# A two-layer HGRN2 / RWKV-7 decoder step: gates, scores and chain in another order, narrower sample products, memory operands split sooner

## The chip, the cores and the metric

One Trainium2 chip, one of its cores. The metric is the device time of one execution in microseconds (us), lower is better. The kernel before takes 2398.97 us (median of 3 runs, 2397.93 to 2401.8).

## What is computed

A trunk of two layers over 1024 prompt tokens and 64 sample tokens (8 sequences of 8), model width 1024, in fp32:

```
layer 0: h = rmsnorm(x); q, f, v, xq, gate = h @ w_in[0]
         HGRN2, 8 heads of 128: S = exp(b_last)*S + (k*exp(b_last-b)) v ;  o = att v + (q*exp(b)) S
layer 1: h = rmsnorm(x); shifted mixes xr, xw, xk, xv, xa = h + (h_prev - h)*mu
         RWKV-7, 16 heads of 64:  S = S*w + (S a) b + v k ;  y = S r
both:    xo = softmax(xq mem_k) mem_v over 256 memory tokens, 4 heads
         x = x + ([mixer | xo] * silu(gate)) @ w_out
mem_k, mem_v = rmsnorm(mem_prompt) @ w_mem_kv  (for the prompt; the samples have caches)
```

Outputs are both token groups after a final norm, the recurrent states and the memory keys and values.

## The kernel before, in words

Big products are made from fp32 operands split into a high and a low part (`split`, L194 to L200: ScalarE (ACT) rounds the high part at L197, VectorE (DVE) or GpSimd (POOL) subtracts at L200), and three matmuls on TensorE (PE) per tile (L216 to L218, or L242 and L1163 to L1165). `load_w` (L203) loads a weight block in one DMA on the SP queue (L209) and splits it. Each call of a tile pool names its buffers; instructions are put into one queue per engine at build time by a list scheduler, which takes program order as the priority and a modelled clock for what is ready. So program order, `tc.high_priority()` and the buffer counts (`BF`, `RB1`) set the order of the work; at run time each engine takes its queue strictly in order.

The stages, by the trace of the profiled execution:

- 0 to 149 us: `build_hT` norms and transposes the tokens of layer 0 (L254 to L269), and the value projection runs beside it: four blocks of 256 columns, each weight block one load and one split by ACT and POOL.
- 149 to 236 us: `memory_kv` (L273). For each of the two layers: transpose the normed memory (L290), scale by DVE (L291), split into `memh` and `meml` (one buffer each; low part by POOL), then eight weight blocks of 128 columns (low part by POOL and DVE in turn) and their products.
- 236 to 858 us: eight HGRN heads (`hgrn_head`, `hgrn_half`). After head h comes the gate of head h-1, then what `FILL[h]` lists: cross attention of the prompt (x), of samples (s), gates 8 to 11 (g). The sample part of a head (L737 to L764) multiplies each sequence's 8 queries with its state (L744), copies the result to SBUF, adds it to the output through a product with the identity (L750), and updates the states in two groups of four sequences: `vx` masks the values of all 64 tokens (L758), one product with 64 rows and 512 columns each (L762), DVE adds (L763).
- 858 to 1050 us: output projection of layer 0 (`out_proj`, L890), its weights loaded at L834.
- 1050 to 1472 us: layer 1's mixes (`blend`, L1038, L1039), low-rank products, and the key, value and receptance projections. `proj` (L1125) runs `key_direction` (L1309 to L1346) of block j after the products of block j+1: it squares, splits (`sh`, `sl`), sums over a head by PE (L1334, L1335) and takes a Newton step of four DVE operations (L1339 to L1342). The value projection opens each PSUM bank by a product with zeros (`zb`, L1156).
- 1472 to 1745 us: `PLAN` and `PLAN2` (L43): twelve gates (g), four cross heads (x), four sample steps (s), and the preparation, scores, tokens, inverse and merge (p, c, t, i, m) of the first blocks.
- 1745 to 2205 us: the loop over nine blocks of `RSEQ` (block 0, the sample block, blocks 1 to 7). Per turn n (L1251): `chain` of block n under high priority, the recurrence itself (L1643 to L1708); `merge_steps` (five, L1560) of block n+1 woven 1 to 2 with `score_steps` (eight, L1461, L1464) of block n+2; then `tokens` (L1489) and `inverse` (L1525 to L1542, a substitution of 15 DVE pairs, L1534 and L1535) of block n+2, `pre` of block n+3, `out` of block n-1, `sample_out`. In turn 0 `sample_in` (L1617) brings the samples' states in, through one PSUM buffer.
- 2205 to 2400 us: the last chain, and the output projection of layer 1.

`rstd_of` (L168) is the norm's reciprocal root: two ACT steps and four DVE operations (L178 to L181) after L173. The lines that set the loop's order:

```
PLAN  "x0 g0 x1 x2 g1 x3 g2 s0 g3 s1 g4 p0 c0 s2 g5 s3"   PLAN2 "t0 i0 m0 p1 g6 g7 g8 g9 g10 g11"
with tc.high_priority():
    x.chain()
ops(n + 1, "values")
weave(seq[n + 1].merge_steps(), seq[n + 2].score_steps(), *WV)      # WV = (1, 2)
ops(n + 2, "tokens", "inverse")
ops(n + 3, "pre")
```

Of the kernel before, what the change touches and what calls it, by code (L numbers as in the profile page):

```python
# [18 lines left out]
D = 1024  # L19
# [24 lines left out]
    "x0 g0 x1 x2 g1 x3 g2 s0 g3 s1 g4 p0 c0 s2 g5 s3", "t0 i0 m0 p1 g6 g7 g8 g9 g10 g11")]  # L44
# [3 lines left out]
WV = (1, 2)  # L48
# [6 lines left out]
BF = dict(hs=3, oT=3, qk=3, zn=3, lt=4, kb=2, tot=2, vv=3, cmp=2, kt=1, S=6, oi=1, kts=1, S0=2, vx=1)  # L55
# [112 lines left out]
def rstd_of(g, ss, n, scale, eps, p=128, sm=None):  # L168
# [9 lines left out]
    nc.vector.tensor_mul(t[:p, :n], y[:p, :n], y[:p, :n])  # L178
    nc.vector.tensor_mul(t[:p, :n], t[:p, :n], v[:p, :n])
    nc.vector.tensor_scalar(t[:p, :n], t[:p, :n], -0.5, 1.5, op0=ALU.mult, op1=ALU.add)  # L180
    nc.vector.tensor_mul(y[:p, :n], y[:p, :n], t[:p, :n])  # L181
# [21 lines left out]
def load_w(g, pool, src, w, kt=KT, elo="pool", raws=2):  # L203
# [5 lines left out]
    nc.sync.dma_start(out=raw, in_=src.rearrange("(k p) c -> p k c", p=128))  # L209
    split(g, hi, lo, raw, elo=elo)  # L210
# [58 lines left out]
def memory_kv(g, mp, sp, kT0, v0):  # L269
# [6 lines left out]
    for i in range(2):  # L276
        x = sp("mx")[:, :D]
        nc.sync.dma_start(out=x, in_=g.mem_prompt[0, 128 * i:128 * i + 128, :])
        norm_rows(g, xs[i], x, 128)
    for layer in range(2):  # L280
        mh = mp.tile([128, KT, MEM], F32R, name="memh", tag="memh", bufs=1)
        ml = mp.tile([128, KT, MEM], F32R, name="meml", tag="meml", bufs=1)
        gb = g.vec[:, g.vo["mg"] + layer * KT:g.vo["mg"] + (layer + 1) * KT]
        for i in range(2):
# [9 lines left out]
            split(g, mh[sl], ml[sl], h)  # L294
# [6 lines left out]
        for j in range(8):  # L301
            w = load_w(g, mp, g.w_mem_kv[layer, :, 128 * j:128 * j + 128], 128, elo="dve" if j % 2 else "pool", raws=3)
# [128 lines left out]
def hgrn_masks(g, c):  # L431
    nc = g.nc
    si = c.tile([128, 32], I32, name="si")
    ti = c.tile([128, 32], I32, name="ti")
    xi = c.tile([128, 32], I32, name="xi")
# [4 lines left out]
    a = c.tile([128, 32], F32, name="ma")  # L440
    b = c.tile([128, 32], F32, name="mb")
    u = c.tile([128, 32], F32, name="mu_")
# [5 lines left out]
    for n, h in enumerate((2, 4, 8, 16)):  # L448
# [3 lines left out]
        nc.vector.tensor_mul(lev[:, n, :], a, u)  # L452
    return base, lev
# [17 lines left out]
def hgrn_layer(ctx, g):  # L471
# [14 lines left out]
    with pool(g, "vw", 2, "right") as vw:  # L486
        with pool(g, "bh", 1) as bh:
            build_hT(g, xsrc, 0, hi, lo, bh)
        for c in range(4):
            wh, wl = load_w(g, vw, g.w_in[0, :, 2048 + 256 * c:2048 + 256 * c + 256], 256)  # L490
# [10 lines left out]
    with pool(g, "xk", 1, "right") as xk:  # L501
# [7 lines left out]
        with pool(g, "hm", 1, "right") as hm, pool(g, "h2", 1, "right") as h2, pool(g, "xc", 1, "right") as xc, \  # L509
# [3 lines left out]
            mbase, mlev = hgrn_masks(g, hm)  # L513
# [459 lines left out]
def rwkv_layer(ctx, g, nn, left):  # L973
# [151 lines left out]
    def proj(col0, cols, xh, xl, dst, fn, after=None, gemm=gemm_ko, raws=2):  # L1125

        late = None
        for j in cols:
# [13 lines left out]
            if late:  # L1142
                after(*late)
# [709 lines left out]
```

## Time and profile before

| | us |
|---|---|
| runs | 2397.93, 2401.8, 2398.97 |
| the profiled execution, and its span from first to last instruction | 2401.76, 2399.8 |
| PE busy, PE weight loads busy | 2238.2, 2001.5 |
| DVE, ACT, POOL busy | 1332.2, 1004.3, 717.7 |
| mean granted clock of TensorE | 0.934 of full speed |

PE is the busiest engine; its busy time also grows where its clock is granted at half speed (1.2 in place of 2.4 GHz), so busy share and granted clock are read together. A matmul record overlaps the next, so the cost of one in a stream is the distance between starts. A row of the timeline gives start, length, engine, line, operation and count, and in brackets the idle time before it and what ended it.

### The profile page before, as it was taken

Reading aid. Unit: us, or ns where it says so; the run is one execution under the profiler, and the core shown is the slowest. Engines: PE = TensorE matmul, PEld = TensorE weight load, DVE = VectorE, ACT = ScalarE, POOL = GpSimd, SP = SyncE. Lnnn points to the kernel's source line nnn. Section 1 sums busy time; section 2 is a strip of 40 time slices with the busy share of each in tenths; the row PEclk is TensorE's granted clock in tenths of the full one; section 3 lists DMA queues with packets and bytes.
Section 4 is the critical chain, followed back from the end, with each engine's and each line's share of the span. In section 5 each row is a group of like instructions: output and inputs, shape, how many; then the busy total and the mean of one; then the engine's idle time right before and its main releaser. Section 6 shows DMA issues by size and latency. Waiting matters only on the chain. (4 is left out here: it accounts for less than half of the span.)

```text
span 2399.8 us, 50625 instructions
## 1 busy us (share of the span) xinstructions
PE 2238.2 (93%) x20980; PEld 2001.5 (83%) x20981; DVE 1332.2 (56%) x2678; ACT 1004.3 (42%) x2240; POOL 717.7 (30%) x559
## 2 busy tenths in 40 slices
PE   5988999999999979989989998999999998899997
PEld 5988888888788858878979998898889987788786
DVE  6113566556775553365796214245576589874643
ACT  4222444444444442266554313344544455444421
POOL 2123121122112310034553412113143255444432
PEclk9998999999999989999999998999986798887999
DMA  5334111223432264215434425145332233312653
GB/s 184 86 96 142 48 56 45 67 70 91 111 87 87 80 193 127 84 41 199 148 122 163 127 93 145 50 103 134 113 108 72 57 101 99 90 55 82 201 158 105
DMA packets 360312, 252.99 MB, mean 105 GB/s; under 512 B 120379, under 2 KB 326403, under 8 KB 360083
## 3 DMA queue, kind: packets, MB, share of 16 engines
q1 hardware_dynamic: 348034, 237.66, 33.3%
q0 software_dynamic: 2544, 7.64, 0.9%
q10 hardware_dynamic: 9504, 4.46, 0.7%
q8 instruction: 165, 2.70, 0.5%
q14 instruction: 65, 0.52, 0.1%
HBM read 172.59 MB, written 77.11 MB: 104 GB/s over the span
## 5 line engine op out<-in xcount | busy, mean ns | idle before, releaser
L200 POOL TENSOR_TENSOR wlo<-wraw,whi 128x1024 fp32r<-128x1024 f32 (+1 forms) x84 | 214.9, 2560 | 646.5 <-ACT whi L197 623.8
L216 PE MATMUL pg<-hi,whi 128*128 128x288 f32 (+3 forms) x800 | 269.1, 336 | 4.5 <-DVE qk L597 2.3
L218 PE MATMUL pg<-hi,wlo 128*128 128x288 f32 (+3 forms) x800 | 266.0, 333 | 0.0
L217 PE MATMUL pg<-lo,whi 128*128 128x288 f32 (+3 forms) x800 | 265.9, 332 | 0.0
L197 ACT ACTIVATE whi<-wraw 128x1024 fp32r<-128x1024 f32 (+1 forms) x92 | 101.0, 1099 | 178.5 <-issue 104.9
L216 PEld LDWEIGHTS pg<-hi,whi 128*128 128x128 f32 x800 | 153.8, 192 | 21.5 <-issue 4.4
L217 PEld LDWEIGHTS pg<-lo,whi 128*128 128x128 f32 x800 | 153.7, 192 | 12.9 <-issue 3.1
L218 PEld LDWEIGHTS pg<-hi,wlo 128*128 128x128 f32 x800 | 153.5, 192 | 11.8 <-issue 2.3
L890 PE MATMUL pout<-owh,bh 128*128 128x512 f32 (+1 forms) x432 | 143.1, 397 | 9.2 <-ACT owh L197 9.2
L890 PE MATMUL pout<-owl,bh 128*128 128x512 f32 (+1 forms) x432 | 142.0, 394 | 0.1
L890 PE MATMUL pout<-owh,bl 128*128 128x512 f32 (+1 forms) x432 | 141.2, 394 | 0.9 <-DVE bl L200 0.9
L216 PE MATMUL pg<-xhi,whi 128*128 128x384 f32 (+2 forms) x392 | 127.6, 325 | 7.1 <-DVE evs L1136 5.0
L218 PE MATMUL pg<-xhi,wlo 128*128 128x384 f32 (+2 forms) x392 | 126.4, 322 | 0.0
L217 PE MATMUL pg<-xlo,whi 128*128 128x384 f32 (+2 forms) x392 | 125.5, 320 | 0.0
L1461 PE MATMUL psc<-AR,BKz 128*128 128x128 f32 x544 | 98.2, 342 | 17.2 <-DVE Q L1464 9.3
L1461 PEld LDWEIGHTS psc<-AR,BKz 128*128 128x128 f32 x544 | 86.7, 244 | 23.1 <-DVE Q L1464 11.0
L890 PEld LDWEIGHTS pout<-owh,bh 128*128 128x128 f32 (+1 forms) x432 | 78.9, 183 | 31.3 <-ACT owh L197 10.8
L197 ACT ACTIVATE bh<-br 128x512 fp32r<-128x512 f32 (+1 forms) x54 | 32.4, 606 | 171.5 <-POOL br L859 84.4
L200 DVE TENSOR_TENSOR bl<-br,bh 128x512 fp32r<-128x512 f32 (+1 forms) x54 | 49.6, 919 | 96.2 <-ACT bh L197 96.2
L890 PEld LDWEIGHTS pout<-owh,bl 128*128 128x128 f32 (+1 forms) x432 | 78.6, 182 | 22.8 <-DVE bl L200 1.8
L242 PE MATMUL pg<-xhi,wlo 128*128 128x384 f32 (+1 forms) x408 | 96.6, 334 | 0.0
L890 PEld LDWEIGHTS pout<-owl,bh 128*128 128x128 f32 (+1 forms) x432 | 78.8, 183 | 21.1 <-DVE owl L200 0.6
(460 smaller groups left out, 6114.9 us busy)
## 6 DMA issues: line engine op xcount, KB each, us to landing
wraw<-in_w_in_dram SPq DMA_DIRECT2D x72, 512.0 KB
oraw<-in_w_out_dram SPq DMA_DIRECT2D x24, 512.0 KB
wraw<-in_w_mem_kv_dram SPq DMA_DIRECT2D x16, 512.0 KB
gT<-evs SPq DMA_DIRECT2D x12, 544.0 KB
vv<-vtk SPq DMA_DIRECT2D x24, 256.0 KB
br<-brT SPq DMA_DIRECT2D x24, 256.0 KB
br<-mixT SPq DMA_DIRECT2D x24, 256.0 KB
gt<-gT SPq DMA_DIRECT2D x24, 256.0 KB
```

The costliest lines, as they stand in the source:

```text
L197: nc.scalar.activation(hi, src, AF.Copy)
L200: (nc.gpsimd if elo == "pool" else nc.vector).tensor_sub(lo, src, hi.bitcast(F32))
L216: nc.tensor.matmul(out, ah, bh, start=first, stop=False)
L217: nc.tensor.matmul(out, ah, bl, start=False, stop=False)
L218: nc.tensor.matmul(out, al, bh, start=False, stop=last)
L242: nc.tensor.matmul(z[:, :n], a[:, k], x(k)[:, t0:t0 + n], start=first, stop=last)
L890: nc.tensor.matmul(ps[c][:p], a[:, k, :p], w[:, 512 * c:512 * c + 512], start=first, stop=last)
L1461: nc.tensor.matmul(ps[:, j], two(BK[:, h, j, 2 * e:2 * e + 2]), two(AR[:, j, 2 * e:2 * e + 2]), start=True, stop=True)
```

## The change

It edits ten places. (1) `rstd_of` and `key_direction` take the Newton step in one DVE operation less. (2) The four weight blocks of layer 0's value projection are loaded and split in four parts. (3) `memory_kv` makes the operands of both layers first, in two buffers each, and all low parts there are DVE's. (4) The HGRN masks move to another pool, and one mask is added. (5) The sample part of a head masks the queries and multiplies 32 columns at a time straight into the output's bank; the state update uses 32 rows at a time and one `vx`. (6) Gate 8 moves from head 6 to head 7, behind gate 9. (7) The `zb` products go. (8) `key_direction` of the last two blocks comes after the mix for the values. (9) `PLAN`, `PLAN2` and `WV` change. (10) The chain loses its priority; inverse goes ahead of tokens, `sample_out` ahead of `pre`; before the loop, tokens, score and inverse of the sample block precede the values of block 0.

```diff
-    "x0 g0 x1 x2 g1 x3 g2 s0 g3 s1 g4 p0 c0 s2 g5 s3", "t0 i0 m0 p1 g6 g7 g8 g9 g10 g11")]
+    "x0 g0 x2 x1 g1 x3 s0 g2 g3 s1 g4 g7 p0 g5 c0 s2 s3", "t0 i0 m0 p1 g6 g8 g9 g10 g11")]
-WV = (1, 2)
+WV = (3, 8)
 # rstd_of
-    nc.vector.tensor_mul(t, y, y)
-    nc.vector.tensor_mul(t, t, v)
-    nc.vector.tensor_scalar(t, t, -0.5, 1.5, op0=ALU.mult, op1=ALU.add)
-    nc.vector.tensor_mul(y, y, t)
+    nc.vector.tensor_mul(t, y, v)
+    nc.vector.scalar_tensor_tensor(t, t, -0.5, y, op0=ALU.mult, op1=ALU.mult)
+    nc.vector.scalar_tensor_tensor(y, t, 1.5, y, op0=ALU.add, op1=ALU.mult)
 # load_w(..., parts=1); the value projection of layer 0 passes parts=4
-    nc.sync.dma_start(out=raw, in_=src.rearrange("(k p) c -> p k c", p=128))
-    split(g, hi, lo, raw, elo=elo)
+    for k in range(0, kt, kt // parts):
+        c = slice(k, k + kt // parts)
+        nc.sync.dma_start(out=raw[:, c], in_=src.rearrange("(k p) c -> p k c", p=128)[:, c])
+        split(g, hi[:, c], lo[:, c], raw[:, c], elo=elo)
 # memory_kv
+    ops = []
     for layer in range(2):
-        mh = mp.tile([128, KT, MEM], F32R, name="memh", tag="memh", bufs=1)
+        mh = mp.tile([128, KT, MEM], F32R, name="memh", tag="memh", bufs=2)
...
-            split(g, mh[sl], ml[sl], h)
+            split(g, mh[sl], ml[sl], h, elo="dve")
+        ops.append((mh, ml))
+    for layer in range(2):
+        mh, ml = ops[layer]
...
-            w = load_w(..., 128, elo="dve" if j % 2 else "pool", raws=3)
+            w = load_w(..., 128, elo="dve", raws=3)
 # hgrn_half, sample part
-    for j in range(2):
-        for b in range(4):
-            o = LS * (4 * j + b)
-            nc.tensor.matmul(pi[:, o:o + LS], s0[:, b, :], qe[:, 512 + o:512 + o + LS], start=True, stop=True)
-    nc.scalar.activation(oi, pi, AF.Copy)
+    nc.vector.tensor_tensor(qm, qe[:, None, 512:].to_broadcast([128, 4, TS]), g.cmask, op=ALU.mult)
     nc.tensor.matmul(po[:, 0, :], atts, vv[:64, 4], start=True, stop=False)
-    nc.tensor.matmul(po[:, 0, :], oi, g.ident, start=False, stop=True)
+    for b in range(4):
+        for r, s0 in zip(rs, S0):          # rs = rows 0..31, 32..63
+            nc.tensor.matmul(po[r, 0, :], qm[:, b, r], s0[:, b, :], start=False, stop=b == 3)
...
-    for j, s0 in enumerate(S0):
-        vx = vv * g.blk of four sequences                          # 64 rows, 4 x 128
-        nc.tensor.matmul(pd, kt, vx, start=True, stop=True)
+    vx = vv * g.bmask                                              # once
+    for r, pd in zip(rs, pds):
+        nc.tensor.matmul(pd, kt[r], vx[r], start=True, stop=True)
 # FILL, heads 6 and 7
-[("g", 8)], [("g", 9), ("g", 10), ("g", 11)]
+[], [("g", 9), ("g", 8), ("g", 10), ("g", 11)]
 # layer 1, keys and values
-    proj(D, range(8), xh, xl, None, None, lambda j, o: key_direction(...))
+    proj(D, range(8), xh, xl, None, None, lambda j, o: key_direction(...), held=held)
     xh, xl = mix(3)
+    for j, o in held:                                              # blocks 6 and 7
+        key_direction(g, kp, j, o, evslot)
-            nc.tensor.matmul(z[:p].rearrange("p a c -> p (a c)"), zb[:, :p], zb, start=True, stop=False)
-                nc.tensor.matmul(z, xh(k)[:, xi], wh[:, k % 4], start=False, stop=False)
+                nc.tensor.matmul(z, xh(k)[:, xi], wh[:, k % 4], start=k == 0 and i % 2 == 0, stop=False)
 # key_direction: n2 = n2*rn; n2 = n2*-0.5*rn; rn = (n2+1.5)*rn  (three operations, four before)
 # the loop
+        ops(1, "tokens")
+        ops(1, "score")
+        ops(1, "inverse")
         ops(0, "values")
-        ops(1, "score", "tokens", "inverse")
...
-            with tc.high_priority():
-                x.chain()
+            x.chain()
             ops(n + 1, "values")
             weave(merge_steps of n + 1, score_steps of n + 2, *WV)
-            ops(n + 2, "tokens", "inverse")
+            ops(n + 2, "inverse")
+            ops(n + 2, "tokens")
+            sample_out, moved up from behind out()
             ops(n + 3, "pre")
```

## Rows read from the trace of the kernel before

**Rows 1.** The page: PE's busy time, its share of the span and its instructions, and the granted clock in 40 slices of the span, in tenths.
```profile
PE 2238.2 (93%) x20980; PEld 2001.5 (83%) x20981; DVE 1332.2 (56%) x2678; ACT 1004.3 (42%) x2240; POOL 717.7 (30%) x559
...
PEclk9998999999999989999999998999986798887999
```

**Rows 2.** Busy time by stage, with a part of the loop at the end: the stretch and its length, busy us (and instructions) of PE, PE's weight loads, DVE, ACT and POOL, then the granted clock, the DMA share and GB/s.
```profile
149.00:236.00 87.00, 70.07 (x498) 65.89 (x496) 27.02 (x52) 28.38 (x42) 32.88 (x22) 0.88 0.50 150
236.00:858.00 622.00, 613.09 (x6490) 523.39 (x6491) 383.43 (x976) 281.14 (x692) 129.75 (x102) 0.98 0.25 73
...
1211.00:1310.00 99.00, 87.96 (x684) 83.46 (x684) 82.10 (x106) 48.42 (x82) 46.57 (x23) 0.98 0.41 143
...
1472.00:1745.00 273.00, 250.84 (x1964) 235.71 (x1962) 119.13 (x250) 121.12 (x292) 57.49 (x44) 0.97 0.38 104
...
1906.00:2205.00 299.00, 280.23 (x4744) 250.72 (x4737) 233.59 (x444) 145.30 (x376) 154.15 (x158) 0.87 0.30 81
...
1980.00:2055.00 75.00, 62.98 (x1020) 55.44 (x1018) 70.40 (x122) 33.13 (x83) 45.73 (x45) 0.87 0.39 103
```

**Rows 3.** The same columns for five stretches in which the clock was granted at half.
```profile
154.60:164.80 10.20, 6.01 (x24) 5.43 (x25) 2.47 (x1) 2.11 (x2) 4.64 (x3) 0.50 0.65 168
192.10:202.40 10.30, 6.22 (x27) 5.92 (x28) 0.75 (x2) 0.73 (x2) 5.29 (x4) 0.50 0.35 115
861.10:878.20 17.10, 6.33 (x12) 3.11 (x13) 9.95 (x13) 7.93 (x10) 2.33 (x3) 0.50 0.98 326
1786.10:1830.50 44.40, 43.89 (x425) 41.01 (x426) 29.27 (x60) 18.08 (x44) 16.32 (x14) 0.50 0.23 61
...
1844.20:1895.40 51.20, 51.20 (x569) 47.91 (x567) 22.52 (x50) 18.58 (x44) 7.47 (x7) 0.50 0.25 62
```

**Rows 4.** The timeline of the start, DVE, POOL, PE and the SP queue (rows of four answers).
```profile
24.63 4.51 DVE L178 TENSOR_TENSOR rt<-ry 128x1 f32<-128x1 f32 x1
...
19.09 12.34 POOL L200 TENSOR_TENSOR wlo<-wraw,whi 128x2048 fp32r<-128x2048 f32 x3 [12.66 <-ACT ry L175]
...
32.67 0.69 PE L262 MATMUL pt<-ident,xs 128*128 128x128 f32 x2 [3.96 <-DVE xs L191]
...
7.10 6.57 SPq L209 DMA_DIRECT2D wraw<-in_w_in_dram  x3
```

**Rows 5.** The timeline of the memory stage, PE and the SP queue.
```profile
156.09 0.58 PE L216 MATMUL pg<-memh,whi 128*128 128x256 f32 x1 [5.13 <-ACT whi L197]
...
196.98 0.58 PE L217 MATMUL pg<-meml,whi 128*128 128x256 f32 x1 [3.57 <-POOL meml L200]
...
150.25 62.25 SPq L209 DMA_DIRECT2D wraw<-in_w_mem_kv_dram  x16
```

**Rows 6.** The heads: PE's timeline, in records, of which a product of fp32 operands leaves two (the eight sample products of one head, the product with the identity, one of its two state products; 15 records of 32 columns in the cross attention of a sample), and the group of the masking `vx` over the whole span (count, busy us, mean ns).
```profile
754.88 1.95 PE L744 MATMUL pi<-qk,S 128*128 128x8 f32 x16
...
760.75 0.43 PE L750 MATMUL pos<-ident,oi 128*64 128x128 f32 x2
...
723.03 1.12 PE L762 MATMUL pds<-vx,kts 64*128 64x512 f32 x2
...
596.59 0.64 PE L415 MATMUL pos<-vc,PTs 128*32 128x128 f32 x15
...
L758 DVE TENSOR_TENSOR vx<-vv,blk 64x512 f32<-64x512 f32 x16 | 12.8, 802 | 1.6 <-DMA vv<-vtk 1.6
```

**Rows 7.** The timeline between the heads and the output projection, PE and the SP queue.
```profile
873.94 1.97 PE L890 MATMUL pout<-owh,bh 128*64 128x512 f32 x4 [9.24 <-ACT owh L197]
...
867.31 1.95 SPq L834 DMA_DIRECT2D oraw<-in_w_out_dram  x4
```

**Rows 8.** Keys and values of layer 1: PE's timeline at the first product with zeros; from the waits of 1150 to 1300 us, PE's for the split squares (us, times, longest); and the Newton step's third operation over the whole span.
```profile
1211.78 0.38 PE L1156 MATMUL pg<-zb 128*128 128x512 bf16 x1 [2.49 <-ACT evs L1138]
...
1212.11 0.28 PE L1164 MATMUL pg<-wlo,xhi 128*128 128x256 f32 x1
1212.23 0.28 PE L1165 MATMUL pg<-whi,xlo 128*128 128x256 f32 x1
...
PE pn L1334 <- ACT sh L197: 11.0, 10, 2.0
...
L1341 DVE TENSOR_SCALAR n<-n 128x384 f32<-128x384 f32 (+1 forms) x24 | 21.9, 914 | 0.6
```

**Rows 9.** PE's timeline in the planned stage: a wait ahead of block 0's scores.
```profile
1635.43 1.99 PE L1461 MATMUL psc<-AR,BKz 128*128 128x128 f32 x10 [3.50 <-DVE nm L326]
```

**Rows 10.** The loop: the substitution's two operations by DVE from 1906 to 2205 us; the longest wait of POOL from 1760 to 2230 us; and DVE's timeline around the state updates of two successive blocks.
```profile
L1534 DVE TENSOR_TENSOR pd<-Xc,L 128x1 f32<-128x1 f32 (+14 forms) x75 | 34.9, 465 | 1.5
...
L1535 DVE TENSOR_REDUCE Xc<-pd 128x1 f32<-128x1 f32 (+14 forms) x75 | 17.6, 234 | 1.3
...
POOL AR L1430 <- PE pas L1617: 36.0, 2, 31.4
...
2154.05 0.69 DVE L1705 TENSOR_TENSOR S<-chainS,S 128x512 f32<-128x512 f32 x1 [0.20 <-PE chainS L1700]
2169.78 0.72 DVE L1573 COPY_PREDICATED N1p<-m,pn 32x512 f32<-32x512 int32 x1 [11.40 <-PE pn L1560]
...
2175.81 0.69 DVE L1705 TENSOR_TENSOR S<-chainS,S 128x512 f32<-128x512 f32 x1
```

**Rows 11.** The norm's third DVE operation over the whole span (count, busy us, mean ns).
```profile
L180 DVE TENSOR_SCALAR rt<-rt 128x1 f32<-128x1 f32 (+4 forms) x71 | 14.2, 204 | 1.3
```

More of the change, by code (lines that the diff above doesn't have):

```diff
@@ L177, in rstd_of @@
     t = sm.tile([128, w], F32, name="rt", tag="rt")
[L178 to L181, printed above, removed]
+    nc.vector.tensor_mul(t[:p, :n], y[:p, :n], v[:p, :n])
+    nc.vector.scalar_tensor_tensor(t[:p, :n], t[:p, :n], -0.5, y[:p, :n], op0=ALU.mult, op1=ALU.mult)
+    nc.vector.scalar_tensor_tensor(y[:p, :n], t[:p, :n], 1.5, y[:p, :n], op0=ALU.add, op1=ALU.mult)
     return y[:p, :n]
@@ L200, in split, with load_w @@
     (nc.gpsimd if elo == "pool" else nc.vector).tensor_sub(lo, src, hi.bitcast(F32))
-def load_w(g, pool, src, w, kt=KT, elo="pool", raws=2):
+def load_w(g, pool, src, w, kt=KT, elo="pool", raws=2, parts=1):
     nc = g.nc
@@ L301, in memory_kv @@
         for j in range(8):
-            w = load_w(g, mp, g.w_mem_kv[layer, :, 128 * j:128 * j + 128], 128, elo="dve" if j % 2 else "pool", raws=3)
+            w = load_w(g, mp, g.w_mem_kv[layer, :, 128 * j:128 * j + 128], 128, elo="dve", raws=3)
             dst = kT[:, j, :] if j < 4 else vT[:, j - 4, :]
@@ L734, in hgrn_half @@
     nc.gpsimd.dma_start(out=g.o_shp[0, 0, hd], in_=S)
-    pi = g.ph["z"].tile([128, TS], F32, name="pi", tag="m")
-    S0 = []
+    qm = mt("qm", 4, TS)
+    nc.vector.tensor_tensor(qm, qe[:, None, 512:].to_broadcast([128, 4, TS]), g.cmask, op=ALU.mult)
+    po = g.ph["z"].tile([64, 1, 128], F32, name="pos", tag="m")
+    nc.tensor.matmul(po[:, 0, :], atts, vv[:64, 4], start=True, stop=False)
+    S0, rs = [], [slice(32 * j, 32 * j + 32) for j in range(2)]
     for j in range(2):
@@ L1123, in rwkv_layer, with proj @@
     tc.keep_in_program_order(nc.scalar.preload_act_table_set("natural_log_exp_and_others"))
-    def proj(col0, cols, xh, xl, dst, fn, after=None, gemm=gemm_ko, raws=2):
+    def proj(col0, cols, xh, xl, dst, fn, after=None, gemm=gemm_ko, raws=2, held=None):
         late = None
@@ L1142, in proj @@
             if late:
-                after(*late)
+                if held is not None and j == cols[-1]:
+                    held.append(late)
+                else:
+                    after(*late)
             late = after and (j, o)
         if late:
-            after(*late)
-    proj(D, range(8), xh, xl, None, None, lambda j, o: key_direction(g, kp, j, o, evslot))
+            if held is not None:
+                held.append(late)
+            else:
+                after(*late)
+    held = []
+    proj(D, range(8), xh, xl, None, None, lambda j, o: key_direction(g, kp, j, o, evslot), held=held)
     xh, xl = mix(3)
+    for j, o in held:
+        key_direction(g, kp, j, o, evslot)
     for c in range(4):
```

62 lines of the change are left out of this document (31 added, 31 removed).

## The prediction, on record before the result

> **What bounds the kernel now.** I read the engines' totals first: PE is busy 93% of the span, DVE 56%, and the granted clock falls below nine tenths in three places: the memory stage, the joint between the heads and the output projection, and much of what comes after 1600 us, most of all around 1800 to 1900 [rows 1]. So the end is set by PE's work, by its idle time, and by the clock it works at. Busy time by stage says which of these counts where [rows 2]. In the memory stage PE is idle 87 - 70.07 = 16.9 us; in the heads only 622 - 613.09 = 8.9 us, so there the length is PE's own work; keys and values of layer 1 leave 99 - 87.96 = 11.0 us; the planned stage 273 - 250.84 = 22.2 us; the loop 299 - 280.23 = 18.8 us, of which 12.0 lie in one block in which DVE is busy 70.40 of 75 us. Last I looked at the stretches at half clock [rows 3]. Three are mostly idle (PE busy 6.01, 6.22 and 6.33 us); the two from 1786 to 1895 us are full: 43.89 of 44.40 and 51.20 of 51.20, with DVE far from busy. At half clock PE's work itself is the bound there.
>
> **The parts, in us of the profiled execution** (2401.8, which is 2.8 above the median of 2398.97).
>
> *Start: -3.* DVE's one-column step of the norm took 4.51 us while POOL ran three 2048-column subtractions in 12.34, 4.11 each, and PE then idled 3.96 us for the tokens [rows 4]. In four parts such a subtraction is estimated at 4.11/4 = 1.03 us, so the step would be held for about 1 us and not 4: -3. The 16 loads in place of 4 stand on SP's queue; three took it 6.57 us, waits included, so 12 more cost it at most 26 us, ahead of the token tiles queued behind. Cover is the 149 us stage, of which the first loads alone matter. Bounds: -4 (the whole gap) to +4 (two parts that PE waits for, 2 x 2.2). Against the change speaks the Trainium skill, DMA: Bandwidth & Descriptors, Bandwidth: one should batch transfers to 1 MiB or more; by it the 1 MiB blocks cut into 256 KB would come later and this term would be nothing or a loss. No row shows the two sizes side by side.
>
> *Memory stage: -11.* With two buffers, layer 1's operands no longer wait for layer 0's products: PE's wait for POOL's `meml`, 3.57 us, goes [rows 5]. The half-clock stretch around it held 6.22 us of PE work, half of which, 3.1, comes back if PE doesn't pause. Of the other idle time, 16.9 - 3.57 = 13.4, I take a third, 4.4: weight low parts now follow one another on DVE and no longer alternate with POOL. Sum 11.1. DVE takes over 8 blocks of 1024 columns and 4 token halves of 1024: 12 x 2.06 = 24.7 us at POOL's pace, beside 27.02 busy of 87; that is covered. Not covered: layer 1's scaling and low part now stand ahead of the first block's low part in DVE's queue, up to 2 x 4.11 = 8.2 us at the same pace, behind the first gap of 5.13. The 16 weight loads on SP start at 150.25 as before. Bounds: all idle time and both half-clock stretches, -16.9 - 6.1 = -23, to 8.2 - 3.6 = +5.
>
> *Heads: -12.* A head's sample products are 16 records in 1.95 us and the product with the identity 0.43 [rows 6]. In their place come 16 records of 32 columns. The nearest row is 15 such records in 0.64 us, spread over four column groups; with the two groups here I estimate twice that, 1.4. Saved 2.38 - 1.4 = 1.0 (between 0.43, as slow as now, and 1.7, as fast as that row). The two state products cost 1.12 each; with 32 rows each, in different row groups, the pair lies between 1.12 and 2.24, and no row shows row groups alone: I take 1.7, saving 0.5. (1.0 + 0.5) x 8 = 12, bounds -23 to -3. DVE loses a `vx` per head (8 x 0.80) and ACT the copy; the masking of the queries adds 256 columns to DVE, at half of `vx`, 0.4. DVE has 239 us free here. Both state products now hold two banks at once, of a pool of two, so the next head's first product there waits for DVE's adds; between heads lies the gate that hides it. The Trainium skill, TensorE: Matmul & The Clock Gate, Part 3, says that products in distinct row groups run concurrently; by it the pair would take about 1.1 and this term be -16 to -17.
>
> *Joint: -5.* PE idles 9.24 us for the split of the output weights, whose loads are issued at 867.31 [rows 7]. Gate 8 behind head 7 gives PE more to do after the last head. Whether the loads come sooner depends on when their space comes free; I take half the gap. Bounds: gap and half of the 6.33 busy at half clock, -12, to +5 where head 6, without its filler, loses the same.
>
> *Keys and values: -8.* A product with zeros put the next records 0.33 apart (1211.78 to 1212.11), the usual step is 0.12 (to 1212.23): 0.21 x 20 = -4.2 [rows 8]. PE waited 11.0 us in ten pieces for the split squares; two of eight blocks now come after the mix, and DVE, busy 82.10 of 99, loses 24 operations of 0.914. I take a third of 11: -4. Bounds -15 to -3.
>
> *Planned stage: 0.* The same work in another order; the longest wait left, 3.50 us for the inverse norm ahead of block 0's scores [rows 9], goes where gate 5 now covers it, and a weight load moved ahead on SP for gate 7 or cross head 2 can be late in turn. Bounds -10 (near half of 22.2) to +8.
>
> *Loop: -6.* The state updates of two blocks start 2154.05 and 2175.81; in between DVE idles 11.40 us for PE's merge of the next block [rows 10]. So the chain waits for merges more than for a place in the queue, and priority is worth little as long as merges come sooner, which weaving three merge steps to eight scores does. The substitution, now ahead of the tokens, is 15 x (465 + 234) ns = 10.5 us of DVE a block. Sample_out moves its loads and DVE work ahead of the next block's loads on SP. I take a third of the 18.8 idle. Bounds: all idle time and a part of the clock (0.87 granted over 299 us is some 78 us at half speed, so 39 lost, of which half), -38, to +30, three of the seven turns late by one substitution.
>
> *Norms: -1.* 71 operations of 0.2 us leave DVE, 14.2 us [rows 11], nearly all beside PE's work.
>
> Sum: -3 - 11 - 12 - 5 - 8 + 0 - 6 - 1 = -46: 2355.8, and by the median 2353.0.
>
> **Rivals.**
> *The low clock lifts.* In the order before, POOL waited 36.0 us (31.4 once) for `sample_in`'s one bank [rows 10], while PE, full, ran at half clock for 44.40 + 51.20 us [rows 3]. With the sample block's tokens, score and inverse ahead of the values, PE's queue meets that stretch in another mix. If the clock stays up, the 95 us of work take 47.5; less what the slower engines then add, some 40 more fall: 2313. For it: PE is never short of work there. Against: nothing in the change removes that work.
> *The chain falls behind (slower).* Without priority, its steps on DVE stand behind the 10.5 us substitution in each of seven turns. It decides once the 11.40 us of slack per turn is taken by merge or DVE work, as in the block with DVE at 70.40 of 75. Price 7 x 10.5 = 73: 2353 + 73 = 2426. Against: in most turns the slack is there.
> *Only removed PE work lands.* Sample products 8, zeros 4.2, the `meml` gap with its clock 6.7: -19. All that depends on order turns into other waits: 2401.8 - 19 - 2.8 = 2380.
> *The order absorbs it.* The scheduler places each instruction again, so removing work can open gaps of the same size; within 4 us of 2399.
>
> **How the numbers follow.** The forecast has 0.50, removed work alone 0.23, the lifted clock 0.12, the chain behind 0.10, no change 0.05. The forecast's terms miss by 4, 13, 9, 9, 6, 9 and 35 at their bounds; squares added give 41, and two thirds of that hold most of it: 2327 to 2379 is its own range. Four parts in five over all cases need the removed-work case with some room above and half of the way to the lifted clock below: 2318 to 2392. About 0.2% (4.8 us) is what a measurement of this kernel can tell from no change. Faster is 0.50 + 0.23 + 0.12 = 0.85, same 0.05, slower 0.10.
>
> **What would show it.** Right: no PE wait for `meml`; memory stage near 76 us; heads near 610 with the sample products under 1.5 us a head and the state products under 1.9; no records of the zeros; the joint's gap near 5; 1745 to 2205 shorter by some 6. The forecast is wrong if the stage from 1745 on moves by over 30 either way (chain or clock), or if the memory stage keeps its length, with DVE's low parts now what PE waits for.

## The result, and the profile after

The changed kernel takes 2338.73 us (median of 4 runs, 2322.15 to 2343.7), the kernel before 2398.45: ratio 0.9737, 95% interval 0.9694 to 0.978, some 60 us less where 46 were forecast. The profiled execution has a span of 2337.4, against 2399.8.

Stages are cut at the same PE instructions in both traces: first transpose of the memory, first product of the heads, first output product, first key product, first and last value product, end of the receptance, first chain product, final states. Measured so, the memory stage before is 76.2 us long and the heads 639.5, not the 87 and 622 of the prediction's windows, so its marks "memory stage near 76" and "heads near 610" stand for some 65 and 627 here.

| stage | before | after | difference | forecast |
|---|---|---|---|---|
| start | 149.0 | 146.4 | -2.7 | -3 |
| memory | 76.2 | 62.1 | -14.1 | -11 |
| heads and joint | 648.7 | 633.9 | -14.8 | -17 |
| output projection 0, mixes | 229.4 | 230.8 | +1.4 | |
| keys | 108.5 | 104.2 | -4.3 | keys and values together -8 |
| values | 125.2 | 126.6 | +1.4 | |
| receptance | 154.8 | 157.5 | +2.7 | |
| planned | 252.6 | 249.8 | -2.7 | 0 |
| loop | 487.9 | 456.7 | -31.2 | -6 |
| end | 167.4 | 169.3 | +1.9 | |

The page after, to set beside [rows 1]: PE's totals, and the clock in 40 slices:

```profile
PE 2178.2 (93%) x20945; PEld 1956.6 (84%) x20945; DVE 1326.3 (57%) x2596; ACT 1004.1 (43%) x2244; POOL 697.2 (30%) x561
...
PEclk9999999999999989999989998999997799889999
```

PE's busy time falls by 60 us, as much as the whole kernel, and the low digits are fewer: the memory stage shows none, and of the deep trough two sevens are left. Half of the gain is in the loop. Busy time by stage of the kernel after (columns as in [rows 2]; the second line is the heads, the third the joint, then keys, values, planned stage and loop):

```profile
146.30:208.40 62.10, 56.43 (x449) 55.52 (x448) 32.94 (x38) 26.01 (x37) 4.15 (x10) 0.95 0.60 171
208.40:829.40 621.00, 599.89 (x6532) 514.42 (x6532) 399.96 (x985) 281.28 (x693) 131.18 (x105) 0.98 0.29 80
829.40:842.40 13.00, 0.04 (x2) 0.01 (x1) 5.82 (x12) 5.95 (x9) 2.32 (x3) 0.57 0.94 341
...
1073.20:1177.40 104.20, 101.34 (x606) 99.87 (x605) 67.89 (x81) 57.15 (x99) 55.33 (x29) 1.00 0.42 148
1177.40:1304.00 126.60, 113.61 (x887) 111.04 (x886) 96.65 (x110) 62.94 (x101) 59.65 (x29) 0.95 0.37 127
...
1461.50:1711.40 249.90, 232.63 (x1880) 218.76 (x1879) 110.95 (x238) 115.99 (x277) 52.02 (x39) 0.99 0.38 102
1711.40:2168.10 456.70, 433.15 (x7052) 391.64 (x7051) 343.45 (x647) 229.71 (x570) 227.61 (x230) 0.86 0.33 91
```

The same stretches of the kernel before, cut at the same instructions:

```profile
149.00:225.20 76.20, 61.11 (x449) 58.13 (x448) 20.86 (x26) 25.88 (x37) 31.79 (x20) 0.87 0.48 139
225.20:864.70 639.50, 626.19 (x6548) 532.39 (x6548) 392.25 (x1008) 285.80 (x702) 133.22 (x107) 0.97 0.27 77
864.70:873.90 9.20, 0.00 (x0) 0.00 (x0) 4.50 (x6) 4.41 (x6) 0.75 (x1) 0.50 0.96 313
...
1103.30:1211.70 108.40, 102.32 (x606) 99.71 (x605) 74.19 (x99) 57.69 (x100) 52.06 (x29) 1.00 0.40 142
1211.70:1337.00 125.30, 114.96 (x904) 109.86 (x905) 96.47 (x116) 62.44 (x102) 60.04 (x29) 0.99 0.38 129
...
1744.40:2232.30 487.90, 459.65 (x7054) 417.11 (x7050) 349.08 (x663) 229.67 (x571) 224.77 (x229) 0.81 0.31 85
```

Read the loop's line by its PE column and its clock column. PE executes the same number of instructions (7054 and 7052) and is busy 26.5 us less; idle time goes only from 28.3 to 23.6; the granted clock goes from 0.81 to 0.86. Half of the time at half clock is lost, as far as PE has work in it, and that half is (1 - clock) x length: 92.7 us before, 63.9 after. I call it the lost time. Without it both loops are as long, 395 and 393. By this reading most of the loop's gain is the clock's. The long half-clock stretches of [rows 3] shrink from 44.4 and 51.2 us to these two, still full of PE work:

```profile
1766.43:1783.50 17.07, 17.07 (x172) 16.23 (x172) 10.07 (x22) 8.56 (x20) 7.31 (x6) 0.50 0.20 50
1793.74:1838.12 44.38, 44.38 (x489) 41.34 (x489) 25.70 (x55) 17.46 (x43) 11.93 (x10) 0.50 0.24 61
```

In the memory stage idle time and clock both count: idle falls from 15.1 to 5.7, and PE busy by 4.7 for the same 449 instructions, since the clock is at 0.95 and not 0.87. PE's wait for `meml` [rows 5] is gone, and the first gap is shorter although DVE has layer 1's operands ahead of it. PE's timeline at the stage's first products:

```profile
153.13 0.38 PE L217 MATMUL pg<-memh,whi 128*128 128x256 f32 x1 [3.11 <-ACT whi L196]
...
155.10 0.43 PE L218 MATMUL pg<-meml,whi 128*128 128x256 f32 x2
```

In the heads PE's work got cheaper by more than forecast. PE's timeline, one head's pair of state products, a wait of the sample part, the eight sample products, and the joint:

```profile
698.09 1.13 PE L773 MATMUL pds<-vx,kts 32*128 32x512 f32 x4
714.47 0.43 PE L754 MATMUL pos<-vv,atts 64*64 64x128 f32 x2 [2.01 <-POOL atts L703]
723.45 1.05 PE L762 MATMUL pos<-S,qm 128*32 128x128 f32 x16
...
842.39 1.97 PE L903 MATMUL pout<-owh,bh 128*64 128x512 f32 x4 [12.96 <-ACT owh L196]
```

Both state products take 1.13 us together, where one took 1.12 [rows 6]; the sample products 1.05, in place of 1.95 and 0.43 for these and the product with the identity. That is 1.1 + 1.3 a head, 19.5 us over eight, and PE's busy time fell by 26.3 with the clock's part. But heads and joint gave only 14.8: idle time in the heads rose from 13.3 to 21.1 and the joint's gap from 9.2 to 13.0. Who makes PE wait, in the heads after (us in all, times, longest):

```profile
PE plev L662 <- DVE qk L689: 4.9, 4, 2.1
PE pos L754 <- POOL atts L703: 3.5, 3, 2.0
```

The second is new: the product with `atts` now opens the bank ahead of the sample products and meets POOL's part of `atts`.

At the joint the gap alone misleads. In both kernels two loads of the output weights go out as the last gate product ends, and four more stand behind other tiles in the queue. SP's timeline before (the four are in [rows 7]) with PE's last state products before, then SP's timeline after:

```profile
858.04 0.81 SPq L834 DMA_DIRECT2D oraw<-in_w_out_dram  x2
...
862.62 2.07 PE L762 MATMUL pds<-vx,kts 64*128 64x512 f32 x2 [1.59 <-DVE vx L758]
```

```profile
829.46 0.82 SPq L847 DMA_DIRECT2D oraw<-in_w_out_dram  x2
...
834.80 2.02 SPq L847 DMA_DIRECT2D oraw<-in_w_out_dram  x4
```

From the first load to the first output product it was 15.9 us before (858.04 to 873.94) and is 12.9 after (829.46 to 842.39). Before, PE had the last head's transposes and state products to do in that time; after, these are done ahead of the gate's end, and nothing covers the wait. So the gap grew although the wait from the loads on got 3 us shorter.

The values' first products now start 0.11 apart, where a product with zeros had put 0.33 between two [rows 8]:

```profile
1177.42 0.28 PE L1181 MATMUL pg<-whi,xhi 128*128 128x256 f32 x1
1177.53 0.28 PE L1182 MATMUL pg<-wlo,xhi 128*128 128x256 f32 x1
```

At the start, the timeline of POOL, DVE and PE:

```profile
15.51 14.20 POOL L199 TENSOR_TENSOR wlo<-wraw,whi 128x512 fp32r<-128x512 f32 x9 [9.11 <-ACT whi L196]
...
23.71 1.23 DVE L178 TENSOR_TENSOR rt<-ry,rv 128x1 f32<-128x1 f32 x1
24.98 1.21 DVE L179 SCALAR_TENSOR_TENSOR rt<-rt,ry 128x1 f32<-128x1 f32 x1
26.22 1.21 DVE L180 SCALAR_TENSOR_TENSOR ry<-rt,ry 128x1 f32<-128x1 f32 x1
30.18 0.15 DVE L178 TENSOR_TENSOR rt<-ry,rv 128x1 f32<-128x1 f32 x1
30.32 1.09 PE L263 MATMUL pt<-ident,xs 128*128 128x128 f32 x8 [2.70 <-DVE xs L190]
```

The one-column step takes 1.2 us and no longer 4.51, but each of the three steps does, beside POOL subtractions of 1.58 us each that follow one another (14.20 us for nine); by 30 us, with POOL through, such a step takes 0.15. PE's gap is 2.70 in place of 3.96.

### The profile page after: what moved, and what is told of

Its sections match the earlier page's. It is cut to its first block, busy times and chain, and to the rows that moved or that the text cites. A ratio compares the mean times of both kernels' runs of the same rounds, so it can differ in the third digit from the quotient of the medians.

```text
span 2337.4 us, 50528 instructions
## 1 busy us (share of the span) xinstructions
PE 2178.2 (93%) x20945; PEld 1956.6 (84%) x20945; DVE 1326.3 (57%) x2596; ACT 1004.1 (43%) x2244; POOL 697.2 (30%) x561
## 3 DMA queue, kind: packets, MB, share of 16 engines
q1 hardware_dynamic: 348226, 237.66, 34.1%
## 5 line engine op out<-in xcount | busy, mean ns | idle before, releaser
L199 POOL TENSOR_TENSOR wlo<-wraw,whi 128x1024 fp32r<-128x1024 f32 (+1 forms) x88 | 199.0, 2269 | 569.7 <-ACT whi L196 532.7
L196 ACT ACTIVATE whi<-wraw 128x1024 fp32r<-128x1024 f32 (+1 forms) x104 | 102.6, 993 | 162.6 <-issue 67.9
L196 ACT ACTIVATE bh<-br 128x512 fp32r<-128x512 f32 (+1 forms) x54 | 32.1, 605 | 161.0 <-POOL br L872 75.2
L689 DVE TENSOR_TENSOR qk<-qk,tot 128x512 f32<-128x512 f32 (+1 forms) x96 | 83.0, 865 | 29.7 <-PE plev L717 18.5
L243 PE MATMUL pg<-xhi,whi 128*128 128x384 f32 (+1 forms) x408 | 97.3, 335 | 0.0
```

The source lines that it names most:

```text
L196: nc.scalar.activation(hi, src, AF.Copy)
L199: (nc.gpsimd if elo == "pool" else nc.vector).tensor_sub(lo, src, hi.bitcast(F32))
L243: nc.tensor.matmul(z[:, :n], a[:, k], x(k)[:, t0:t0 + n], start=first, stop=last)
L689: nc.vector.tensor_tensor(v, v, w[:, :, :, None].to_broadcast([128, 2, n // (2 * h), h]), op=ALU.mult)
```

## The experiments

Theories at the outset. **Clock:** the loop's gain is half-clock time that went, brought by the loop's new order. **Waits:** the loop's gain is waits that went. **Elsewhere:** the clock's share came from the stages ahead. All kernels below are the changed one with an edit; each ratio is against the kernel before, measured beside it. In the code excerpts, lines that begin with # are in words. "Stage" figures are of one profile each; over the ten or eleven kernels whose edit lies elsewhere the memory stage varies from 60.9 to 62.3, heads and joint from 633.9 to 637.3, keys and values together from 230.6 to 231.8, the start from 143.8 to 147.4.

### The loop as a whole

```diff
-WV = (3, 8)
+WV = (1, 2)
-            x.chain()
+            with tc.high_priority():
+                x.chain()
 # and: values of block 0 first; tokens ahead of inverse; sample_out behind out
```

> The changed kernel with its whole loop put back in the order before (chain under priority, weave 1 to 2, tokens ahead of inverse, sample_out behind out, values ahead of the sample block's tokens, score and inverse); all other edits stay. Clock theory: the stretch from the first chain product to the final states goes from 457 back to some 488 us, +31; of this some 26 are PE busy time of the same instructions and the half-clock time in it goes from 130 to about 188 us; the whole kernel near 2370 in place of 2339. Rival, waits: the 31 come back mostly as PE idle time (idle from 24 to over 40 us) with the half-clock time as it is. Rival, other edits: the loop keeps 457 to 465 us, the gain came in from earlier stages' phase of the clock.

Measured: 2364.7 us, ratio 0.9855 (0.9817 to 0.9894), 1.2% above the changed kernel by their ratios. The loop is 487.1 us, with PE busy and clock as before the change:

```profile
1712.00:2199.10 487.10, 461.54 (x7084) 415.19 (x7080) 344.60 (x647) 230.68 (x571) 225.37 (x229) 0.80 0.32 86
```

Idle time is 25.6, the clock 0.80; less the 97.4 us lost to it, the loop is 390 us long, as in the other two. So the loss came back as lost time and not as waits, with nothing but the loop's order edited.

The profile is of one execution, but every execution has its span and granted clock on record, and span less lost time can be had for each. It is 2206 to 2217 us in the four executions of this kernel and 2210 to 2220 in eight of the changed one, against 2235 to 2248 in 19 of the kernel before. The lost time is 131 to 161, 102 to 131 and 141 to 159. So the old order of the loop costs lost time and, as far as can be told, nothing else; and of the some 60 us that the whole change gains about half is lost time and half is work and waits gone. Note also that one and the same program's executions differ by up to 29 us of lost time, as much as the loop's gain: a single profile says little here.

### One piece of the loop at a time

```diff
 # priority_back
-            x.chain()
+            with tc.high_priority():
+                x.chain()
 # weave_back
-WV = (3, 8)
+WV = (1, 2)
 # values_first
-        ops(1, "tokens"); ops(1, "score"); ops(1, "inverse"); ops(0, "values")
+        ops(0, "values"); ops(1, "score", "tokens", "inverse")
 # tokens_first; sample_out also goes behind out() again, as before
-            ops(n + 2, "inverse"); ops(n + 2, "tokens")
+            ops(n + 2, "tokens", "inverse")
```

> The changed kernel with the chain under high priority again. Theory that priority is the piece that counts (it lets small chain products go ahead of merges that the next block needs): +15 to +25 us. Rival, the forecast's reading (the chain waits for merges and not for its place in the queue): within 5 us. Rival, that losing priority costs: 5 to 20 us faster than the changed kernel.

> The changed kernel with merges and scores woven 1 to 2 again, not 3 to 8. Theory that sooner merges shorten the turn: +5 to +15 us, in turns 1 to 7. Rival: the two weaves put nearly the same products in the same order (five steps and eight), within 5 us.

> The changed kernel with the values of block 0 ahead of the sample block's tokens, score and inverse again. Theory that this shifts work out of the long half-clock stretch of turn 0: half-clock time in the first 130 us of the loop from 68 back to about 100 us, +10 to +17 us in all. Rival: the same work is only moved by a place, within 5 us.

> The changed kernel itself, as the measure for the others on its chip: 0.974 of the kernel before; loop near 457 us with some 130 at half clock, if the clock falls the same way each time. If the half-clock time of the same program differs between profiles by tens of us, single profiles say less than the medians.

> The changed kernel with tokens ahead of inverse and sample_out behind out, as before. Since the whole loop put back cost 30 us, priority and values-first some 5 us each in the loop and the weave gave 17 back, clock theory: this is the piece with the largest share, loop +15 to +30, with 30 to 60 us more at half clock after sample_in. Rival, pieces don't add (the list scheduler makes another order from any edit): within 8 us, and the half-clock time moves either way.

| kernel | us | ratio (95%) | loop, PE idle in it, us |
|---|---|---|---|
| changed kernel, again | 2334.58 | 0.9737 (0.9698 to 0.9777) | 458.9, 21.5 |
| priority back | 2345.38 | 0.9799 (0.9774 to 0.9825) | 461.6, 28.4 |
| values first | 2345.7 | 0.9795 (0.9773 to 0.9817) | 463.9, 26.0 |
| tokens first | 2338.15 | 0.9761 (0.9716 to 0.9805) | 460.0, 29.1 |
| weave back | 2319.37 | 0.9695 (0.9667 to 0.9723) | 439.4, 23.9 |

No single piece brings the 30 us back. With priority or with the values first the kernel is about 0.6% slower, by intervals that touch or overlap the changed kernel's; in the loop they add 3 to 7 us, with a little more idle time (28.4 and 26.0 against 21.5 and 23.5). So the theories that priority or the place of the tokens carries the loop fell. Priority alone costs something that is not the clock: its four executions, less the lost time, take 2223 to 2226 us, where the changed kernel takes 2210 to 2220. The whole loop put back has the priority too and doesn't show this, so it hangs on the rest of the order. The weave of 3 to 8 gains nothing; 1 to 2 was even the fastest kernel of the study. The loop's lines of this kernel:

```profile
1709.00:2148.40 439.40, 415.54 (x7051) 376.85 (x7051) 338.65 (x647) 228.84 (x577) 225.00 (x230) 0.90 0.35 94
```

### How far one order fixes the clock

```diff
-    proj(D, range(8), ..., lambda j, o: key_direction(...), held=held)
+    proj(D, range(8), ..., lambda j, o: key_direction(...))          # and WV = (1, 2)
```

> The changed kernel with the weave of before (1 to 2) and the last two blocks' key directions not held back: two pieces that measured better undone. If pieces add: keys and values together 2 us shorter than with the weave alone, loop near 440, the whole 0.967 to 0.970 of the kernel before, faster than both. Rival, the edit ahead of the loop gives the loop another order and with it another share of half clock: loop anywhere from 440 to 470, whole up to 0.98.

Measured: 2333.51 us, 0.975 (0.9726 to 0.9774). This was meant as the best of all, and became a control by accident: leaving out the hold changes no instruction's place on PE (in both traces PE's list is the same but for 14 of 20,945 records that start almost together; the two runs of the changed kernel itself differ in that way too). Yet the loop took 451.6 us at a clock of 0.88, and the run time is 14 us above that of the weave alone:

```profile
1710.40:2162.00 451.60, 425.85 (x7053) 385.86 (x7053) 338.07 (x647) 228.21 (x575) 226.05 (x230) 0.88 0.34 91
```

So one and the same order on PE gives a loop that differs by 12 us, nearly all of it clock (lost 43.9 and 54.2 us; the rest 395.5 and 397.4). Whether the study, the buffers or chance did it wasn't tried; the changed kernel gave 0.9737 in both of its studies.

Kernels whose loop has no edit show the same, and that the clock of the loop also moves with edits far ahead of it. In fill_back (below; one gate moved in the heads) PE's order in the loop differs from the changed kernel's in 78 of 7,050 places, all in the first tenth; in stages_2 (below) the edits ahead also reordered the loop:

```profile
1718.30:2165.70 447.40, 425.95 (x7054) 384.08 (x7051) 340.37 (x648) 230.67 (x571) 228.00 (x230) 0.87 0.34 93
...
1732.90:2202.70 469.80, 450.04 (x7051) 403.06 (x7050) 335.84 (x663) 230.22 (x570) 225.94 (x231) 0.84 0.32 89
```

With 449.4 in stages_1 and 456.7 and 458.9 in the changed kernel, the loop as it stands in the change takes 447 to 470 us. So the third theory, elsewhere, isn't wholly out: edits ahead are worth up to 13 us in the loop, either way. Differences of 0.6% between kernels here are not worth an explanation, and neither weave can be called the better; the 1.2% of the whole loop is twice that. Its 487 us lie 17 above the longest of these loops, and it came with a clock, 0.80 to 0.81, that none of the other orders had.

### What the clock goes with

```diff
+                for _ in range(4):                              # behind each of sample_in's 16 groups
+                    nc.tensor.matmul(pf[:, 128:], g.zb, g.zb as 128 x 384, start=True, stop=True)        # dense_fill
+                    nc.tensor.matmul(pf[:32, 128:160], g.zb[:32, :32], g.zb[:32, :32], ...)              # small_fill
```

> The changed kernel with four added products of 128 by 128 weights and 384 bf16 columns of zeros behind each of sample_in's 16 groups of small products, into unused columns of the same bank: 64 products, about 0.16 us each at full clock, 10 us of work that nothing needs. Clock theory (the half clock goes with what PE is given there: 32- and 64-row products of few columns): half-clock time up to the end of sample_in falls from 60 to 66 us to under 30, and that part of the loop gets no longer or even shorter by some 5 us in spite of the added work. Rival, the clock has nothing to do with the sort of products: half-clock time as before, part longer by 10 to 20 us.

> Control for dense_fill, since any added instruction gives another order: the same 64 added products in the same places, but 32 by 32 weights and 32 columns. Clock theory: half-clock time up to the end of sample_in stays at 50 to 75 us. If it falls here as with the wide products, it was the new order or the pauses and not the sort of products.

Measured: 2352.61 us (0.9817, 0.9782 to 0.9851) and 2350.15 us (0.9814, 0.977 to 0.9858). The part of the loop up to the end of `sample_in`, for the kernel before, the changed one, the wide and the small products, and in the part with the wide ones the group of these:

```profile
1744.40:1891.10 146.70, 143.56 (x1785) 133.53 (x1781) 88.69 (x174) 64.23 (x154) 48.73 (x52) 0.67 0.32 83
```

```profile
1711.40:1830.20 118.80, 114.39 (x1477) 105.62 (x1475) 76.31 (x154) 53.37 (x126) 43.75 (x48) 0.75 0.35 92
```

```profile
1714.90:1852.00 137.10, 133.76 (x1652) 115.83 (x1648) 84.12 (x168) 58.37 (x138) 49.01 (x52) 0.75 0.33 90
```

```profile
1713.00:1833.00 120.00, 114.62 (x1523) 105.30 (x1521) 67.77 (x129) 49.30 (x117) 40.18 (x46) 0.73 0.34 89
```

```profile
L1640 PE MATMUL pas<-zb 128*128 128x384 bf16 x64 | 16.4, 389 | 0.0
```

Wide products didn't raise the clock (0.75 with and without them); they made the part 18 us longer. They are busy for 16.4 us themselves, not the 10 that I had expected, in part because five of their 16 groups ran at half clock; and the part holds 111 other records more, so it isn't the same work. My reading, that the clock falls because PE is given narrow products, is not borne out; since the added operands were zeros, products with other data aren't excluded. What is left is a correlation, and not a full one. In the loops of 13 of the 14 traces every half-clock stretch of over 20 us begins while `sample_in` is woven with scores and merges. In loop_before two more, of 27.3 and 34.1 us, come some 200 us after its end, the second with PE full of chains, scores and merges:

```profile
2085.60:2119.70 34.10, 34.10 (x423) 31.69 (x422) 15.96 (x38) 9.68 (x23) 5.60 (x6) 0.51 0.06 17
```

So `sample_in` isn't needed for it. The cause stays open.

### The other stages

```diff
 # stages_1
-load_w(..., 256, parts=4)
+load_w(..., 256)
-split(g, mh[sl], ml[sl], h, elo="dve"); load_w(..., 128, elo="dve", raws=3)
+split(g, mh[sl], ml[sl], h); load_w(..., 128, elo="dve" if j % 2 else "pool", raws=3)
-nc.tensor.matmul(pd, kt[r], vx[r], ...)         # 32 rows, one vx
+nc.tensor.matmul(pd, kt, vx, ...)               # 64 rows, a vx for each
-[], [("g", 9), ("g", 8), ("g", 10), ("g", 11)]
+[("g", 8)], [("g", 9), ("g", 10), ("g", 11)]
+nc.tensor.matmul(z, zb[:, :p], zb, start=True, stop=False)
 # stages_2: Newton steps of four operations, PLAN and PLAN2 as before, and
 # memh, meml: one buffer in place of two, each layer made and used in turn
-nc.tensor.matmul(po[r, 0, :], qm[:, b, r], s0[:, b, :], ...)
+nc.tensor.matmul(pi[:, o:o + LS], s0[:, b, :], qe[...], ...); oi; product with ident
-proj(..., key_direction, held=held)
+proj(..., key_direction)
 # fill_back: the one line of FILL alone
```

> The changed kernel with one edit undone in each of five stages; each is read in its own stage. Start: weight blocks in one part again, +3 us by the forecast, 0 if the gain is the shorter norm alone. Memory: two buffers stay, but POOL makes the operands' low parts and every second weight low part again: forecast 4 us longer than 62.1; rival, the buffers alone gave it, within 1.5; rival, DVE's share is the greater part, 8 us and more. Heads: state products with 64 rows and two masks again: +4 of 8 x 0.5 by the forecast (2.24 in place of 1.7 us a head); +9 if row groups run side by side; 0 if not at all. Joint: gate 8 behind head 6 again, gap 9 in place of 13 us, the heads by as much longer. Values: products with zeros again, +4 by the forecast.

> The changed kernel with the other edit undone in each stage. Start: Newton step of four operations, +0 to +1. Memory: one buffer for the operands and layer 1's made behind layer 0's products, low parts by DVE: +7 to 62.1 by the forecast (gap 3.6 and its half clock); rival, under 2. Heads: sample products of 8 columns and the identity again: +8 (1.0 a head) by the forecast, up to +13. Keys and values: last two blocks' directions not held, four Newton operations: +4 over both stages by the forecast; rival, no more than 1, since held work only moves its waits into the values. Planned stage: old order, within 3 us.

> The changed kernel with gate 8 behind head 6 again; all else stays. Read in heads plus joint (633.9 us in the changed kernel, gap before the output projection 12.97). Theory that the move costs: the gap falls to some 10 us and heads plus joint get 3 to 8 us shorter, since with both this and the wide state products undone the stretch grew by only 2.7 while the products alone cost PE 12. Rival, the move helps as the forecast said (5 us): heads plus joint 5 us longer. Rival, no difference within 2.

stages_1 took 2342.62 us and stages_2 2371.53 (one run each), fill_back 2339.99 (0.9776, 0.9742 to 0.981). By stage, against the changed kernel:

| stage | edit undone | measured | forecast |
|---|---|---|---|
| start | four parts | 150.6, +4.2 | +3 |
| start | Newton of three | 145.3, none | 0 to 1 |
| memory | DVE for low parts | 65.2, +3.1 | +4 |
| memory | two buffers, both layers first | 68.3, +6.2 | +7 |
| heads, joint | narrow sample products | 648.7, +14.8 | +8 |
| heads, joint | gate 8 behind head 7 | 639.5, +5.6 | +5 |
| heads, joint | gate 8 and narrow state products | 636.6, +2.7 | +9 |
| keys, values | products with zeros gone | 234.2, +3.4 | +4 |
| keys, values | hold, Newton of three | 228.7, -2.1 | +4 |
| planned | order | 252.5, +2.7 (receptance and planned stage together vary from 404 to 411 elsewhere) | 0 |

The memory stage of stages_1 and stages_2 (first lines) and the heads of stages_2:

```profile
150.60:215.80 65.20, 58.96 (x451) 56.19 (x449) 20.54 (x26) 25.91 (x37) 33.44 (x22) 0.92 0.56 163
```

```profile
145.30:213.60 68.30, 58.37 (x450) 56.83 (x448) 33.29 (x38) 25.89 (x37) 4.15 (x10) 0.90 0.54 156
213.60:849.40 635.80, 619.02 (x6548) 531.64 (x6546) 396.43 (x998) 284.76 (x701) 131.91 (x105) 0.97 0.28 78
```

Start, memory and the zeros came out near the forecast in size; the two memory edits give 9.3 alone and 14.1 together. Without DVE's low parts, though, idle time grows only from 5.7 to 6.2 us, and PE's busy time by 2.5, at a lower clock. The hold is worth nothing: weave_back_not_held, without it, needs 231 us for keys and values, as all do that have it (230.6 to 231.8), so the 2.1 us gained in stages_2 stay unexplained. Undoing the narrow sample products puts 19.1 us of PE work back and the stage takes 14.8 of them. The state products are the surprise: cheaper by 1.1 us a head in the trace, but with gate 8 behind head 6 the stage is 636.6 with the wide and 639.5 with the narrow ones. And 636.6 lies within the 633.9 to 637.3 of the kernels edited elsewhere: both edits undone cost nothing that can be told. The timelines of SP and PE at the last head of fill_back, then of stages_1, show where such a saving can go:

```profile
824.52 0.81 SPq L847 DMA_DIRECT2D oraw<-in_w_out_dram  x2
828.22 1.11 PE L792 MATMUL pot<-ident,on 128*128 128x128 f32 x4 [3.73 <-DVE rt L179]
...
830.79 2.08 PE L773 MATMUL pds<-vx,kts 32*128 32x512 f32 x4 [0.36 <-ACT kts L767]
845.92 1.54 PE L903 MATMUL pout<-owh,bh 128*64 128x512 f32 x3 [13.06 <-ACT owh L196]
```

```profile
830.77 0.81 SPq L846 DMA_DIRECT2D oraw<-in_w_out_dram  x2
...
852.40 1.97 PE L902 MATMUL pout<-owh,bh 128*64 128x512 f32 x4 [9.85 <-ACT owh L196]
```

With the gates used up, PE waits 3.73 us for the last norm, and then 13.06 for the weights. From the first load of the output weights to the first output product it takes 21.4 us here and 21.6 in stages_1, with the narrow and with the wide state products. So the 3.2 us by which PE is sooner through with the narrow ones, at this head, come back as gap (13.06 in place of 9.85). With gate 8 behind head 7 the same way from the first load takes 12.9. What became of the saving in the other heads the runs don't show.

## Why the prediction was right, and where it wasn't

**Right in the total** (2338.7 within 2318 to 2392, 60 us gained against 46), and in part by luck. Of the 62.4 us between the profiled spans, the stages outside the loop gave 31.2 where 40 were forecast, and the loop gave 31.2 where 6 were: the clock in the loop made up for what the others lacked. The prediction's own mark for failure, the stage from 1745 us on moving by over 30 us, was met: -31.

- *Start and zeros:* size and mechanism held; each was undone in its own stage, in one profile. The Trainium skill, DMA: Bandwidth & Descriptors, Bandwidth, says that transfers should be batched to 1 MiB or more; by it the four parts of 256 KB would have cost time. The runs go the other way: with whole blocks the start takes 150.6 us (stages_1), with parts 143.8 to 147.4.
- *Memory:* the size held, and PE's wait for `meml` is gone as forecast. DVE's low parts paid by the clock and hardly by idle time, of which I had booked 4.4. The planned stage's -2.7 is within its spread. One reading of mine was wrong: of the three half-clock stretches that I called mostly idle, the two of the memory stage have PE busy for 59 and 60% (6.01 of 10.20, 6.22 of 10.30).
- *Heads:* right in the sum, wrong inside. I took 1.0 and 0.5 us a head and measured 1.3 and 1.1, on PE. The Trainium skill, TensorE: Matmul & The Clock Gate, Part 3, says that products in distinct row groups run concurrently; by it the pair would take about 1.1, and the trace agrees: 1.13. What I left out is the price: I called the stage PE-bound because idle time was small, and so booked every saved microsecond as gain. 26.3 us of PE's busy time, 19.5 of it by cheaper products, gave 14.8 with the joint, the rest turning into waits (idle +7.8, gap +3.8). Undone by themselves, the narrow sample products are worth 14.8; for the state products no gain of time is shown.
- *Joint:* the size was right (5.6 us by fill_back) and the step wrong: the gap did not shrink, it grew from 9.2 to 13.0. The gate covers the wait for the last norm and part of the time from the loads on instead.
- *Keys and values:* the zeros are worth 3.4, as forecast. The failing step is "two of eight blocks now come after the mix": PE's order is the same with and without the hold (weave_back and weave_back_not_held), and so is the time. PE's wait for the split squares fell only from 11.0 us [rows 8] to this, and other waits grew:

  ```profile
  PE pn L1354 <- ACT sh L196: 8.8, 8, 2.2
  ```

  Besides, the values' clock fell from 0.99 to 0.95, which loses 5 us more than before: -2.9 in all and not -8.
- *Loop:* -6 forecast from idle time, -4.7 found there; that term was sound. The other -26.5 are the clock, which I had priced within the bounds and as a rival of 0.12, in one stretch only. The part to the end of `sample_in` loses 48 us before and 30 after; the rest of the loop 44 and 34. So the stretch that the rival named gave about half of its 40 us, and the later turns gave 10. The rival also read POOL's wait of 36.0 us as one for `sample_in`'s bank; the row [rows 10] names `AR`, which those products read, and that the bank is behind it isn't shown.
- *The chain falls behind:* it did not. With priority back the kernel is no faster (0.9799 against 0.9737), and PE idles more.

## What to carry to other kernels

Multiply (1 - granted clock) by the length of each stage before anything else: where PE is full and the clock low, that product is a term of its own, in this loop larger than all of PE's idle time (92.7 us against 28.3), and an order of instructions can win or lose it without a change of work. Once cheaper PE work leaves PE waiting at the next engine's pace, only part of it is gain, so book savings in a "PE-bound" stage against the slack of the engine that feeds it. And before crediting a piece of a reordering, learn how far kernels with the same order differ: here 12 us between two of them, and up to 29 us of lost time between executions of one program. A reading of the clock needs several executions, and span less lost time is the steadier number.

## What the runs showed of the hardware

- Two products of 32 rows, 128 weight columns and 512 fp32 columns, in different row groups, took 1.13 us together; one product of 64 rows took 1.12.
- One and the same list of PE instructions ran a loop in 439.4 us at a granted clock of 0.90 and in 451.6 at 0.88, while the length less the lost time stayed within 2 us. In eleven of the twelve profiles without added products it lies between 389 and 397; with priority back it is 406.
- PE was busy for 51.20 of 51.20 us at half clock before, and for 44.38 of 44.38 after.
- In eight executions the changed kernel lost 102 to 131 us to the clock, while span less lost time stayed between 2210 and 2220.
- 64 added products of 128 by 128 by 384 zeros did not raise the granted clock of their stretch (0.75 and 0.75).
- A one-column DVE operation took 1.2 us beside running POOL subtractions of 512 columns (1.58 each), 4.51 beside those of 2048 (4.11 each), and 0.15 with POOL idle.
